# Attention's output projection as seven products over token and head halves, in a two-layer retention and stick-breaking decoder on one Trainium2 core

## The chip, the core and the metric

The kernel runs on one core of one Trainium2 chip. A core has five engines that work side by side, each through its own instructions in order: TensorE (PE in the profile, with its weight loads as PEld), VectorE (DVE), ScalarE (ACT), GpSimd (POOL) and SyncE (SP), which here only issues DMAs. Matrix products land in eight PSUM banks of 128 x 512 float32; all else lies in SBUF, or in DRAM, from where DMAs bring it. The metric is the time on the device in microseconds, as a median of several runs. A profile is one execution, so its numbers belong to that execution's own time.

## What is computed

The input is 1024 tokens of width 1024. Layer 0 is retention with four heads, layer 1 is stick-breaking attention with eight heads of 256 values. Only the end of layer 1 matters here (cut from the reference):

```python
u = rms_norm(h, sb_norm_pre[j])
proj = u @ sb_w_in[j]
q, g = jnp.split(proj, [SB_QK_WIDTH], axis=-1)
q = split_heads(q, SB_HEADS).astype(jnp.float32)
o = stick_breaking_attention(q, k_shared, v_shared)
o = merge_heads(o).astype(h.dtype) * jax.nn.silu(g)
y = o @ sb_w_out[j]                      # 1024 x 2048 by 2048 x 1024
h = h + rms_norm(y, sb_norm_post[j])
```

`stick_breaking_attention` gives each token a sum over all earlier tokens, so a token of the upper half looks at both halves, and token 0 gets zero. `y = o @ sb_w_out` is the output projection.

## The kernel before

Float32 products are made of three matmuls: each operand is split into a high part (ACT rounds it to the fast format) and a low part (DVE subtracts), and `mm3` adds high x high, high x low and low x high in a PSUM bank. So each operand of a product costs a half on ACT and a half on DVE before PE can use it.

Tokens go in two halves `t` (0 lower, 1 upper) of 512. The attention heads go in pairs `p` (0 to 3). `CPair` holds one pair of heads for one token half; `rows(hh)` makes the scores of one head (sigmoids, a scan and a product on DVE), `mix(hh)` transposes the weights on PE, splits them and multiplies them by the values into two banks `po`, and its last step `gate` multiplies by the gate.

Ahead of the heads stand six groups of input products, K, Q, V0, G0, V1 and G1 (`Group`). Each computes a 1024 x 1024 block by seven products of 48 matmuls over halves of tokens and inputs (numbers 1 to 7; number 2 of all six groups is made first). V1 and G1 are values and gates of heads 4 to 7.

The output projection of layer 1 is made per pair. The gate's result is split into tiles `oT` in SBUF, and `outproj` (lower tokens, result with the output's columns on the partitions) or `outproj_rows` (upper tokens, result in rows) multiplies it by the pair's quarter of the weights: 8 banks of 4 blocks of the inner dimension, 3 matmuls each, 96 per call. The sums over pairs are kept in DRAM (`y_d`): loaded into `f`, added to a bank, stored again. Each call stands beside a later head pair, so that PE has these matmuls while ACT and DVE work on the head. The first pair of the lower half stands beside G1's last two products, the second pair beside nothing, and the last pair's call, upper tokens, ends the kernel. `c_post` norms the lower half with statistics from PE and writes it; `finish` norms the upper half by rows as its banks come.

The output projection of layer 0 is different: `AOut` makes it from seven products of four quarters each way (the Winograd form of Strassen's method). A product has four units `i`; a unit has a weight tile `whl` and an operand tile `op`, both of 128 x 2 x 1024, which `weights` and `operand` make from one to three quarters loaded from DRAM as `raw`, added or subtracted on DVE and split; PE uses a unit for 24 matmuls.

The order in time is not that of the code: all instructions are recorded, and a planner (`Plan`) with a cost for each places them on the engines, within the dependencies and the numbers of buffers. `merge` sets which work is recorded beside which. Nearly all instructions carry one line of a recorder (L229 in the profile), so they are told apart by the names of their tiles: `pma`, `pmb`, `pz` and `po` are PSUM banks (two each), `wraw`/`raw` loaded weights, `whl` split weights, `A` weights of attention, `AT` their split transposes, `ko`, `v`, `vo` keys, queries and values, `sg` gates, `f` scratch.

Of the kernel before, what the change touches and what calls it, by code (L numbers as in the profile page):

```python
# [10 lines left out]
F32 = mybir.dt.float32  # L11
# [446 lines left out]
def trunk(ctx, tc, xT, wts, gains, trig, ident_in, cols, grow_in, out):  # L458
# [64 lines left out]
    def unit(idx, gain=None):  # L523

        w = S("whl", [2, 1024], F32R)
        for c in range(2):
            o = 512 * c
            raw = S("wraw", [512])
            dma(raw[:], wts[idx, :, o:o + 512])
            for a, b, g in [(p[0] - o, p[1] - o, p[2]) for p in gain if o <= p[0] < o + 512] if gain else [(0, 512, None)]:  # L530
                split((w[:, 0, o + a:o + b], w[:, 1, o + a:o + b]), raw[:, a:b], g)
        return w

# [34 lines left out]

    def proj(base, xh, typ, evac, gain=None):


        box = {}
        get = ahead(4, lambda kk: unit(base + kk, gain(kk) if gain else None))

        def chunk(j):
            kk, half, c = j // 4, j // 2 % 2, j % 2
            i = 2 * kk + c
            if j == 0:
                box["b"] = [PS(n) for n in banks4]
            w, x, banks = get(kk), xh[i], box["b"]  # L580
            if j % 4 == LEAD:
                get(kk + 1)
            for b in (2 * half, 2 * half + 1):
                bl = slice(128 * b, 128 * b + 128)
                if typ == "N":
                    n = slice(512 * c + 128 * b, 512 * c + 128 * b + 128)
                    mm3(banks[b][:], w[:, 0, n], w[:, 1, n], x[:, 0, :], x[:, 1, :], i == 0, i == 7)
                else:
                    n = slice(512 * c, 512 * c + 512)
                    mm3(banks[b][:], x[:, 0, bl], x[:, 1, bl], w[:, 0, n], w[:, 1, n], i == 0, i == 7)  # L590
            if j >= 12 and c:
                evac(2 * half, banks)

        return Chunks([lambda j=j: chunk(j) for j in range(16)], lambda: get(0))

    def outproj(base, oT, y_d, first, acc=None, tags=None, hold=None):

        box = {}
        get = ahead(4, lambda ng: unit(base + ng))

        def sum_so_far(c):
            if hold is None:
                y = S("f2", [512])
            else:
                if c < 4:
                    hold.append(S("S", [2, 512]))
                y = hold[c % 4][:, c // 4]
            if not first:
                dma(y[:], y_d[c])
            return y  # L610
        sums = ahead(8, sum_so_far)

        def chunk(j):
            c, half = divmod(j, 2)
            ng, b = divmod(c, 2)
            w = get(ng)
            if j % 4 == LEAD:
                get(ng + 1)
            if half == 0:
                box["p"] = PS(tags[c % 4] if tags and c < 4 else banks4[c % 4])  # L620
                sums(c)
                if not first:
                    sums(c + 1)
                    sums(c + 2)
            p, y = box["p"], sums(c)
            for e in (2 * half, 2 * half + 1):
                n = slice(256 * e + 128 * b, 256 * e + 128 * b + 128)
                mm3(p[:], w[:, 0, n], w[:, 1, n], oT()[e][:, 0, :], oT()[e][:, 1, :], e == 0, e == 3)
            if half == 0:
                return  # L630
            if first:
                A_.activation(y[:], p[:], AF.Copy)
            else:
                V.tensor_tensor(y[:], p[:], y[:], ALU.add)
            if hold is None:
                dma(y_d[c], y[:])
            if acc is not None:
                sumsq(acc, y[:], c, G if hold is None else V)

        def pre():  # L640
            get(0)
            if not first:
                sums(0)
                sums(1)

        return Chunks([lambda j=j: chunk(j) for j in range(16)], pre)

    def outproj_rows(base, oT, y_d, first, done=None):

        box = {}  # L650
        get = ahead(4, lambda u: unit(base + u))

        def sum_so_far(c):
            y = S("f2", [512])
            if not first:
                dma(y[:], y_d[c])
            return y
        sums = ahead(8, sum_so_far)

        def chunk(j):  # L660
            c, half = divmod(j, 2)
            nh, tb = divmod(c, 4)
            w = get(2 * nh + half)
            if tb == 2:
                get(2 * nh + half + 1)
            if half == 0:
                box["p"] = PS(banks4[c % 4])
                sums(c)
                if not first:
                    sums(c + 1)  # L670
                    sums(c + 2)
            p, y, tl = box["p"], sums(c), slice(128 * tb, 128 * tb + 128)
            for e in range(2):
                x, n = oT()[2 * half + e], slice(512 * e, 512 * e + 512)
                k = 2 * half + e
                mm3(p[:], x[:, 0, tl], x[:, 1, tl], w[:, 0, n], w[:, 1, n], k == 0, k == 3)
            if half == 0:
                return
            if first:
                A_.activation(y[:], p[:], AF.Copy)  # L680
            else:
                V.tensor_tensor(y[:], p[:], y[:], ALU.add)
            if done:
                done(nh, tb, y)
            else:
                dma(y_d[c], y[:])

        def pre():
            get(0)
            if not first:  # L690
                sums(0)
                sums(1)

        return Chunks([lambda j=j: chunk(j) for j in range(16)], pre)
# [80 lines left out]
    y_d = [[rec.tile(dr, [128, 512], F32, f"y{t}{c}", dram=True) for c in range(8)] for t in range(2)]  # L775
# [6 lines left out]
    v_d = [[[DRAM(f"v{t}{p}{b}", F32R) for b in range(4)] for p in range(NPAIR)] for t in range(2)]  # L782
    g_d = [[[rec.tile(dr, [128, 512], F32, f"g{t}{p}{f}", dram=True) for f in range(4)] for p in range(NPAIR)] for t in range(2)]
# [285 lines left out]
    class AOut:  # L1069

        def __init__(self, base, hold, acc):
            self.base, self.hold, self.acc = base, hold, acc
# [33 lines left out]
        def operand(self, n, i):  # L1106

            def load(t, half):
                raw = S("raw", [1024])
                dma(raw[:], o_d[t][2 * half + i // 2][i % 2][:])  # L1110
                return raw

            x = S("op", [2, 1024], F32R)
            if n in (1, 2, 3):
                a = load(*{1: (1, 0), 2: (1, 1), 3: (0, 1)}[n])
            elif n in (5, 7):
                a, b = (load(1, 0), load(0, 0)) if n == 5 else (load(0, 1), load(0, 0))
                V.tensor_tensor(a[:], a[:], b[:], ALU.subtract)
                if n == 5:
                    self.x[i] = a  # L1120
            else:
                a, b = self.x[i], load(0, 1) if n == 6 else load(1, 1)
                V.scalar_tensor_tensor(a[:], a[:], -1.0, b[:], ALU.mult, ALU.subtract)
            split(self.pieces(x), a[:])
            return x

        def put(self, t, j, b, y):
            sumsq(self.acc[t], y, 4 * j + b, V)
# [26 lines left out]
        def y(self, t, j, b):  # L1155
            if self.hold[t][b] is None:
                self.hold[t][b] = S("S", [2, 512])
            return self.hold[t][b][:, j]

        def chunk(self, n, i, kk):  # L1160
# [6 lines left out]
            w, x = self.get(at)  # L1167
            banks = self.banks[5 if n == 3 else n]
            sl = slice(512 * kk, 512 * kk + 512)
            for b in range(4):  # L1170
                cl = slice(512 * kk + 128 * b, 512 * kk + 128 * b + 128)
                mm3(banks[b][:], w[:, 0, cl], w[:, 1, cl], x[:, 0, sl], x[:, 1, sl], n != 3 and i + kk == 0, i == 3 and kk == 1, goes_on=n == 3)
            if i == 3 and kk == 1:
                for b in range(4):
                    self.done(n, b, banks[b])
# [340 lines left out]
    class CPair:  # L1516
        def __init__(self, t, pr):
            self.t, self.pr, self.base, self.off = t, pr, 112 + 16 * t + 4 * pr, HT * t
            self.oT = [None] * 4
            self.A = [[], []]  # L1520
            self.kq = [None] * 4

        def out(self, y_d, acc=None, done=None):
# [398 lines left out]
```

## Time and profile before

| | |
|---|---|
| median of three runs | 1617.39 us (1615.33 to 1618.29) |
| the profiled execution, its own time | 1614.99 us |
| its span, first to last instruction | 1613.2 us |
| mean granted TensorE clock | 0.999 |
| DRAM traffic | 405.85 MB, 252 GB/s over the span |
| DMA landing, median | `wraw` 5.0 us, `ko` 6.1 us, `raw` 7.2 us |

The profile's views used here: the page (busy time of each engine, and 40 slices of the span in tenths), the waits (who waited for whom), windows (busy time in given stretches), the chain of work that ended last, the groups of equal instructions (count, busy us, mean ns of one, idle time before), the timeline, and the DMA issues. The ends of matmuls are modelled, so the start of one to the start of the next tells their pace.

### The profile page before, as it was taken

To read this page: it belongs to the slowest core of one execution; us is meant where nothing else is said; L and a number is where in the kernel's file an instruction comes from. 1 tells how busy PE (TensorE), PEld (TensorE's weight loads), DVE (VectorE), ACT (ScalarE), POOL (GpSimd) and SP (SyncE) were. 2 spreads that over 40 slices of the span, in tenths; PEclk is the share of its full clock that TensorE was granted. 3 is DMA by queue.
4 is the path that set the end of the run, shared out by engine and by line. 5 is a ranking of instruction groups with operands and counts; after the bars stand their busy time and mean duration, and the time that the engine had idled before them with its cause. 6 is when DMAs were issued, how large, how long until landed. Compare 5 with 4: busy or idle time off the path is not lost.

```text
span 1613.2 us, 22605 instructions
## 1 busy us (share of the span) xinstructions
PE 1600.7 (99%) x7538; PEld 1327.9 (82%) x7538; DVE 1275.5 (79%) x1942; ACT 829.1 (51%) x1490; POOL 238.4 (15%) x306
## 2 busy tenths in 40 slices
PE   9999999999999999999999999999999999999997
PEld 7888888888888888888788888888888888888886
DVE  7998779787667787899978765757758886878997
ACT  7643432323566665545665554545545645545543
POOL 0000024240122323300000000000002211212410
PEclk9999999999999999999999999999999999999999
DMA  8775636478557887885676967659787878787893
GB/s 284 245 254 173 228 111 229 137 270 291 178 194 272 302 320 270 306 309 185 223 271 222 347 227 280 243 176 317 259 318 263 272 250 302 258 297 266 286 301 129
DMA packets 187573, 405.85 MB, mean 252 GB/s; under 512 B 21057, under 2 KB 21697, under 8 KB 187457
## 3 DMA queue, kind: packets, MB, share of 16 engines
q1 hardware_dynamic: 187456, 404.41, 71.9%
q8 instruction: 59, 0.97, 0.2%
q14 instruction: 58, 0.47, 0.1%
HBM read 291.08 MB, written 113.25 MB: 251 GB/s over the span
## 4 chain that ended last, share of the span: by engine, by line
PE 74%; DVE 2%; issue 1%; POOL 1%; ACT 1%; DMA 0%; DVEq 0%; SPq 0%; POOLq 0%; ACTq 0%
PE pma L229 21%; PE pmb L229 20%; PE po L229 18%; PE pz L229 15%; DVE f L229 1%; DMA wraw<-in_wts_dram 0%; DVE S L229 0%; POOL f L229 0%; POOL small L229 0%; DVE acc L229 0%; ACT f L229 0%; DVE small L229 0%; ACT sgn L229 0%; DVE wraw L229 0%; ACT whl L229 0%
## 5 line engine op out<-in xcount | busy, mean ns | idle before, releaser
L229 ACT ACTIVATE whl<-wraw 128x512 fp32r<-128x512 f32 (+1 forms) x328 | 194.3, 626 | 240.3 <-PE po L229 73.0
L229 DVE TENSOR_TENSOR whl<-wraw,whl 128x512 fp32r<-128x512 f32 x328 | 228.5, 722 | 108.8 <-ACT whl L229 108.0
L229 PE MATMUL pma<-whl,xh 128*128 128x512 f32 x480 | 125.3, 393 | 0.4 <-ACT whl L229 0.4
L229 PE MATMUL pmb<-whl,xh 128*128 128x512 f32 x480 | 122.7, 389 | 0.0
L229 POOL TENSOR_SCALAR_AFFINE_SELECT f<-f 128x128 f32<-128x128 f32 x64 | 32.9, 531 | 504.5 <-ACT f L229 493.7
L229 PE MATMUL pma<-xh,whl 128*128 128x512 f32 x408 | 105.7, 392 | 0.2 <-ACT xh L229 0.2
L229 PEld LDWEIGHTS pmb<-whl,xh 128*128 128x128 f32 x480 | 90.0, 188 | 18.9
L229 PE MATMUL pmb<-xh,whl 128*128 128x512 f32 x408 | 104.6, 391 | 0.0
L229 PEld LDWEIGHTS pma<-whl,xh 128*128 128x128 f32 x480 | 88.6, 188 | 18.3 <-ACT whl L229 0.8
L229 PE MATMUL pz<-ko,ko 128*128 128x512 f32 (+3 forms) x480 | 101.7, 331 | 0.0
L229 POOL TENSOR_TENSOR f<-f,f 128x512 f32<-128x512 f32 x32 | 56.0, 1759 | 248.5 <-DVE f L229 222.5
L229 DVE SCALAR_TENSOR_TENSOR wraw<-wraw,gn,wraw 128x512 f32<-128x512 f32 x96 | 70.4, 748 | 24.9 <-ACT wraw L229 18.8
L229 PEld LDWEIGHTS pma<-xh,whl 128*128 128x128 f32 x408 | 75.9, 188 | 17.0 <-ACT xh L229 0.8
L229 PEld LDWEIGHTS pmb<-xh,whl 128*128 128x128 f32 x408 | 76.5, 188 | 16.2 <-issue 0.5
L229 PE MATMUL pma<-op,whl 128*128 128x512 f32 x336 | 89.5, 396 | 0.0
L229 PE MATMUL pmb<-op,whl 128*128 128x512 f32 x336 | 86.1, 390 | 0.0
L229 PEld LDWEIGHTS pz<-ko,ko 128*128 128x128 f32 x480 | 77.4, 189 | 9.9 <-DVE AT L229 0.9
L229 PE MATMUL pma<-whl,oT 128*128 128x512 f32 x312 | 82.2, 397 | 0.5 <-ACT whl L229 0.5
L229 PE MATMUL pmb<-whl,oT 128*128 128x512 f32 x312 | 80.4, 392 | 0.0
L229 ACT ACTIVATE AT<-pz 128x512 fp32r<-128x512 f32 (+1 forms) x96 | 45.9, 491 | 65.0 <-PE pz L229 64.8
L229 PE MATMUL po<-xh,whl 128*128 128x512 f32 x312 | 79.2, 389 | 0.0
L229 PE MATMUL pz<-xh,whl 128*128 128x512 f32 x312 | 79.1, 389 | 0.0
(213 smaller groups left out, 3588.2 us busy)
## 6 DMA issues: line engine op xcount, KB each, us to landing
wraw<-in_wts_dram SPq DMA_DIRECT2D x495, 256.0 KB, 5.0
v<-v SPq DMA_DIRECT2D x64, 512.0 KB, 6.0
ko<-kq SPq DMA_DIRECT2D x40, 512.0 KB, 6.1
raw<-in_wts_dram SPq DMA_DIRECT2D x36, 512.0 KB, 7.2
raw<-o SPq DMA_DIRECT2D x36, 512.0 KB, 7.3
kq<-v SPq DMA_DIRECT2D x32, 512.0 KB, 6.3
y<-f SPq DMA_DIRECT2D x56, 256.0 KB, 2.9
f<-y SPq DMA_DIRECT2D x48, 256.0 KB, 4.8
```

Of the source, the lines that this page charges most:

```text
L229: f(*[_real(a) for a in o.args], **{k: _real(v) for k, v in o.kw.items()})
```

## The change

The projection of layer 1 becomes one call of the class that layer 0 used, renamed `Out`: seven products over token halves and head halves (heads 0 to 3 lower, 4 to 7 upper). `gate` no longer splits its result; it writes it to DRAM (`oc_d`), from where `operand` loads quarters. The running sums `y_d`, `outproj`, `outproj_rows` and `c_post` go. Operands are `turned`, so that both token halves come out in rows, and `finish(t)` now norms both; for token 0 it sets the factor to zero. The last product, number 2, runs bank by bank (`last`) where the others run all four banks for each unit.

The heads are recorded in another order: the eight lower head calls (two halves of tokens, heads 0 to 3) stand beside four products each of V1 and G1 (numbers 6, 7, 4, 5), and the eight upper ones beside products 1, 5, 3 and 6 of the projection, two each. Products 7, 4 and 2 come after the last head.

```diff
-    def outproj(base, oT, y_d, first, acc=None, tags=None, hold=None):
...
-    def outproj_rows(base, oT, y_d, first, done=None):
...
+    oc_d = [[[DRAM(f"oc{t}{p}{n}", F32) for n in range(2)] for p in range(NPAIR)] for t in range(2)]
...
-    class AOut:
+    class Out:
...
-                dma(raw[:], o_d[t][2 * half + i // 2][i % 2][:])
+                dma(raw[:], self.o_d[t][2 * half + i // 2][i % 2][:])
...
+            if n == 2 and self.turned:
+                x = [hl("AT") for _ in range(2)]
+                for kk in range(2):
+                    split((x[kk][:, 0], x[kk][:, 1]), a[:, 512 * kk:512 * kk + 512])
+                return x
...
+        def multiply(self, n, i, kk, b, bank):
+            w, x = self.get(self.units.index((n, i)))
+            w, x = w[:, :, 512 * kk:512 * kk + 512], x[kk]
+            l, r = (x, w) if self.turned else (w, x)
+            cl = slice(128 * b, 128 * b + 128)
+            mm3(bank[:], l[:, 0, cl], l[:, 1, cl], r[:, 0, :], r[:, 1, :], n != 3 and i + kk == 0, i == 3 and kk == 1, goes_on=n == 3)
+            if i == 3 and kk == 1:
+                self.done(n, b, bank)
...
+        def last(self):
+            first = self.units.index((2, 0))
+
+            def chunk(b, i):
+                if b == 0:
+                    self.get(first + i)
+                    self.get(first + i + 1)
+                if i == 0:
+                    self.banks[b] = PS(banks4[b])
+                for kk in range(2):
+                    self.multiply(2, i, kk, b, self.banks[b])
+            return Chunks([lambda b=b, i=i: chunk(b, i) for b in range(4) for i in range(4)], lambda: self.get(first))
...
             def gate():
+                o = S("S", [2, 512])
                 for e in range(2):
-                    j = 2 * hh + e
-                    g = box["g"][e]
-                    V.tensor_tensor(g[:], box["po"][e][:], g[:], ALU.mult)
-                    if e == 0:
-                        self.o = S("oT", [2, 2, 512], F32R)
-                    x = self.oT[j] = self.o[:, e]
-                    split((x[:, 0, :], x[:, 1, :]), g[:])
+                    V.tensor_tensor(o[:, e], box["po"][e][:], box["g"][e][:], ALU.mult)
+                dma(oc_d[self.t][self.pr][hh][:], o[:].rearrange("p a b -> p (a b)"))
...
-    def c_post(t, y_d, acc):
...
-    def finish():
+    def finish(t):
...
+            if t + tb == 0:
+                seen = S("small", [1])
+                V.tensor_scalar(seen[:], ident[:, 0:1], -1.0, 1.0, ALU.mult, ALU.add)
+                V.tensor_tensor(r[:, 0:1], r[:, 0:1], seen[:], ALU.mult)
...
-        heads = [(0, 0), (0, 1), (1, 0), (0, 2), (1, 1), (0, 3), (1, 2), (1, 3)]
-        fill = [None, (0, 0), (0, 1), (1, 0), (0, 2), (1, 1), (0, 3), (1, 2)]
...
+        heads = [(0, 0), (0, 1), (1, 0), (1, 1), (0, 2), (0, 3), (1, 2), (1, 3)]
+        P = {h: CPair(*h) for h in heads}
+        seq = [(h, hh) for h in heads for hh in range(2)]
...
+        for at, first in ((4, 0), (5, 4)):
+            n = order[at]
+            go(groups[at].chunks(n[0]), None if first else lambda: [(P[seq[0][0]].rows(0), 0, 0)])
+            for k in range(4):
+                go(groups[at].chunks(n[k + 1]), lambda k=k: head(first + k))
+            go(groups[at].chunks(n[5]))
+        turns, done = zip(*[finish(t) for t in range(2)])
+        Y = Out(112, oc_d, True, lambda t, j, b: S("f2", [512])[:], lambda t, j, b, y: done[t](j, b, y))
+        for k, n in enumerate((1, 5, 3, 6)):
+            for half in range(2):
+                go(Y.chunks(n)[4 * half:4 * half + 4], lambda k=k, half=half: head(8 + 2 * k + half))
+        go(Y.chunks(7), lambda: [(turns[0], 0, 1)])
+        go(Y.chunks(4), lambda: [(turns[1], 0, 0)])
+        go(Y.last())
```

Where instructions come to stand is seen from the built program's order, which has no times. First PE at the very end. Before, the last two banks (`pmb`), each 12 matmuls from two weight tiles and the last pair's two `oT` tiles:

```order
L229 MATMUL pmb_15879<-whl_15705,oT_15471 128x512 x6
L229 MATMUL pmb_15879<-whl_15728,oT_15755 128x512 x6
L229 MATMUL pmb_15902<-whl_15705,oT_15471 128x512 x6
L229 MATMUL pmb_15902<-whl_15728,oT_15755 128x512 x6
```

Now the very last bank alone, over four weight tiles and the eight half operands of product 2:

```order
L229 MATMUL pmb_15637<-whl_15341,AT_15357 128x512 x3
L229 MATMUL pmb_15637<-whl_15341,AT_15370 128x512 x3
L229 MATMUL pmb_15637<-whl_15391,AT_15413 128x512 x3
L229 MATMUL pmb_15637<-whl_15391,AT_15419 128x512 x3
L229 MATMUL pmb_15637<-whl_15452,AT_15469 128x512 x3
L229 MATMUL pmb_15637<-whl_15452,AT_15475 128x512 x3
L229 MATMUL pmb_15637<-whl_15485,AT_15515 128x512 x3
L229 MATMUL pmb_15637<-whl_15485,AT_15519 128x512 x3
```

A bank now takes 24 matmuls in a row where it took 12.

Second, SP where the second head of the upper tokens' third pair is loaded: its own keys, its queries and the lower tokens' keys, all into `ko`. Before (`y_91` is a running sum's store, `wraw` and `vo` are weights and values for later):

```order
L229 DMA wraw_14178<-in_wts_dram 128x512
L229 DMA ko_14189<-kq_242 128x1024
L229 DMA y_91<-f_13784 128x512
L229 DMA ko_14219<-kq_244 128x1024
L229 DMA ko_14237<-kq_226 128x1024
L229 DMA vo_14260<-v_259 128x512
```

Now the same three loads (queries, lower keys, own keys), among them the store of the gated head before (`oc_272`):

```order
L229 DMA raw_13857<-oc_270 128x1024
L229 DMA ko_13880<-kq_228 128x1024
L229 DMA oc_272<-S_13873 128x1024
L229 DMA ko_13914<-kq_210 128x1024
L229 DMA ko_13927<-kq_226 128x1024
L229 DMA v_13937<-v_257 128x1024
```

The two loads of keys now stand behind a store that waits for DVE's gating of a head. On PE, between that head's last product (`po`) and the first use of the keys, now stand 32 matmuls of 512 columns and 8 transposes, the last of them these:

```order
L229 MATMUL pz_13916<-ident,A_13888 128x128
L229 MATMUL po_13951<-AT_13947,vo_13768 128x512
L229 MATMUL po_13954<-AT_13947,vo_13768 128x512
L229 MATMUL pz_13959<-ko_13914,ko_13880 128x512 x3
L229 MATMUL pz_13966<-ko_13927,ko_13880 128x128 x3
```

The last two rows are the scores that use the loaded keys.

Third, DVE at the end of product 4, where its first banks (`pma_15238`, `pma_15248`) are read and the operands of product 2 are made:

```order
L229 SCALAR_TENSOR_TENSOR A_15102<-A_15102,col_15444,A_15090 128x1024
L229 SCALAR_TENSOR_TENSOR A_15068<-A_15068,col_15446,A_15124 128x1024
L229 TENSOR_TENSOR whl_15452<-raw_15397,whl_15452 128x1024
L229 SCALAR_TENSOR_TENSOR f_15480<-pma_15238,f_14957 128x512
L229 SCALAR_TENSOR_TENSOR f_15487<-pma_15248,f_14970 128x512
L229 TENSOR_TENSOR AT_15469<-raw_15416,AT_15469 128x512
L229 TENSOR_TENSOR AT_15475<-raw_15416,AT_15475 128x512
L229 TENSOR_TENSOR whl_15485<-raw_15437,whl_15485 128x1024
```

Before, DVE near its end read a bank, scaled it, and wrote a row block for each bank in turn, with nothing else between:

```order
L229 TENSOR_TENSOR f_15659<-pma_15837,f_15659 128x512
L229 TENSOR_TENSOR A_15780<-f_15659,A_15481 128x512
L229 RECIPROCAL col_15872<-small_15866 128x1
L229 SCALAR_TENSOR_TENSOR A_15780<-A_15780,col_15872,A_15535 128x1024
L229 TENSOR_TENSOR f_15678<-pma_15857,f_15678 128x512
```

Now the lower tokens' finish (`A_15102`, `A_15068`), the reading of product 4's banks and the halves of product 2's operands share DVE.

More of the change, by code (lines that the diff above doesn't have):

```diff
@@ L567, in ahead @@
         return get
[L569 to L594, printed above, removed]
@@ L596, in outproj @@
-    def outproj(base, oT, y_d, first, acc=None, tags=None, hold=None):
[L598 to L646, printed above, removed]
@@ L648, in outproj_rows @@
-    def outproj_rows(base, oT, y_d, first, done=None):
[L650 to L694, printed above, removed]
@@ L1166, in chunk @@
                     self.banks[n] = [PS(tag) for tag in banks4]
[L1167 to L1169 removed]
             for b in range(4):
[L1171 to L1175, printed above, removed]
+                self.multiply(n, i, kk, b, self.banks[5 if n == 3 else n][b])
         def chunks(self, *which):
@@ new lines, in run @@
+        for at, group in enumerate(groups[:4]):
+            go(group.chunks(*order[at]), (lambda: [(late[2:], 0, 16)]) if at == 0 else None)
+        for at, first in ((4, 0), (5, 4)):
[5 more added lines that the diff above has]
+        turns, done = zip(*[finish(t) for t in range(2)])
```

179 lines of the change are left out of this document (47 added, 132 removed).

## The prediction

> **What bounds the kernel now.** I read the page first, for the busy shares and the slices.
>
> ```profile
> span 1613.2 us, 22605 instructions
> PE 1600.7 (99%) x7538; PEld 1327.9 (82%) x7538; DVE 1275.5 (79%) x1942; ACT 829.1 (51%) x1490; POOL 238.4 (15%) x306
> PE   9999999999999999999999999999999999999997
> PEclk9999999999999999999999999999999999999999
> ```
>
> PE has work in every slice but the last, at a clock that is never throttled. A busy PE need not be at its peak, so next come the waits of PE (what it waited for, total us, times, longest) and windows in stretches where no head runs (us; then busy us and instruction count of PE, PEld, DVE, ACT, POOL; clock, DMA share, GB/s).
>
> ```profile
> PE pz L229 <- DVE onesr L229: 1.4, 1, 1.4
> PE po L229 <- ACT sgn L229: 1.1, 3, 0.4
> PE pma L229 <- ACT whl L229: 1.0, 2, 0.5
> ...
> 960.00:1000.00 40.00, 40.00 (x178) 33.13 (x177) 28.51 (x45) 21.13 (x37) 0.00 (x0) 1.00 0.94 347
> 1120.00:1200.00 80.00, 80.00 (x354) 66.16 (x354) 50.74 (x78) 40.90 (x70) 0.00 (x0) 1.00 0.82 293
> ```
>
> All waits of PE come to 4.0 us in 1613. In 80 us 354 matmuls start, one per 0.226 us. The chain that ended last (start us, length, what) has the same pace in its tail, and the price of a transpose:
>
> ```profile
> 1582.09 0.90 PE pz L229 x8
> 1582.99 5.51 PE pma L229 x24
> 1588.49 5.44 PE pmb L229 x24
> ```
>
> 24 matmuls of 512 columns take 5.44 us, 0.227 each; eight 128x128 transposes take 0.90, 0.113 each. So the time is a sum of matmuls that follow each other, with a head and a tail. A change is worth what it takes off that sum, unless PE starts to wait.
>
> **The change on PE.** The old projection has eight head pairs (four, each for two token halves), each with 8 banks of 12 matmuls: 768. Seven products of 96 are 672. Removed: 96 x 0.227 = 21.8 us. Lower tokens now end in rows, as upper ones did, so the residual of that half is turned: 32 more transposes x 0.113 = 3.6 us. Its old statistics go:
>
> ```profile
> L229 PE MATMUL pz<-ones,acc 128*128 128x1 f32 x56 | 6.7, 241 | 0.3 <-DVE acc L229 0.3
> L229 PE MATMUL pz<-sgn,onesr 128*128 128x512 f32 x10 | 3.8, 392 | 0.0
> ```
>
> Four products with ones, 8 of these 56 records at 6.7/56 = 0.12 us: 1.0; and two of `sgn,onesr` at the pace of 512 columns, 0.45. PE's sum falls by 21.8 + 1.0 + 0.45 - 3.6 = **19.6 us**. The heads, with their scores, transposes and value products, are the same sixteen, and only stand elsewhere.
>
> The Trainium skill has a rule that would make this smaller: "TensorE: Matmul & The Clock Gate", section "Back-to-back issue gap", gives about 131 ns for a 512-column matmul in a sustained stream. By it the 96 would be worth 12.6 us, and the time about 1607. This trace does not agree: it has 227 ns, 24 times in a row.
>
> **The tail.** Rows of the timeline (start us, length, engine, operation, count, idle before):
>
> ```profile
> 1599.21 5.60 PE L229 MATMUL pmb<-whl,oT 128*128 128x512 f32 x24
> 1605.10 0.75 DVE L229 SCALAR_TENSOR_TENSOR f<-f,col,A 128x512 f32<-128x512 f32 x1
> 1605.77 0.68 DVE L229 TENSOR_TENSOR f<-pmb,f 128x512 f32<-128x512 f32 x1
> 1607.83 1.41 DVE L229 SCALAR_TENSOR_TENSOR f<-f,col,A 128x512 f32<-128x512 f32 x2
> ```
>
> PE is done at 1604.81, but the last bank is read 0.96 us later, since DVE still writes the rows of the bank before; banks end 2.7 us apart (12 matmuls), and a bank's chain on DVE and ACT takes 1609.24 - 1605.77 = 3.5. In the changed order a bank has 24 matmuls, 5.4 us, so that chain is over. The rest (the same chain, the same two 256 KB stores) stays: **-0.9 us**.
>
> **Waits that may come.** (a) Loads. The order of the instructions has two loads of K behind the store of a gated head, and 32 matmuls of 512 columns and 8 transposes, 32 x 0.227 + 8 x 0.113 = 8.2 us, from that head's last product to their use. What has to fit in: two gate multiplications, the loads' own issue, the landing:
>
> ```profile
> L229 DVE TENSOR_TENSOR sg<-po,sg 128x512 f32<-128x512 f32 x32 | 21.2, 681 | 1.2 <-PE po L229 1.1
> L229 SPq DMA_DIRECT2D ko<-kq x34: 320/406/973, 1200.9 to 1514.1; - x34
> DMA to landing us min/median/max: 3.6/5.8/9.1
> ```
>
> 2 x 0.68 + 0.41 + 5.8 = 7.6 by the median, and 10.9 by the longest landing. So from nothing (0.6 to spare) to 2.7 late; nearer to the median, I take **+0.5**. The store itself is queued between them, another 0.4. Behind the waiting store SP also holds value loads, used more than 10 us later. Before, the same load had 28 us: the store ahead of it, `y_91`, belongs to a bank that ended that much PE work earlier.
>
> (b) DVE. Per instruction:
>
> ```profile
> L229 DVE TENSOR_TENSOR whl<-wraw,whl 128x512 fp32r<-128x512 f32 x328 | 228.5, 722 | 108.8 <-ACT whl L229 108.0
> L229 DVE TENSOR_TENSOR whl<-raw,whl 128x1024 fp32r<-128x1024 f32 x28 | 34.2, 1225 | 6.1 <-ACT whl L229 6.1
> L229 DVE TENSOR_TENSOR op<-raw,op 128x1024 fp32r<-128x1024 f32 x28 | 34.0, 1218 | 6.8 <-ACT op L229 6.7
> L229 DVE TENSOR_TENSOR raw<-raw,raw 128x1024 f32<-128x1024 f32 x24 | 29.4, 1224 | 0.0
> L229 DVE TENSOR_TENSOR oT<-sg,oT 128x512 fp32r<-128x512 f32 x32 | 22.8, 719 | 0.1
> L229 DVE TENSOR_TENSOR f<-pma,f 128x512 f32<-128x512 f32 x62 | 42.2, 687 | 13.2 <-PE pma L229 13.0
> ```
>
> New: 28 + 24 long halves and 32 long sums and differences, 84 x 1.22 = 102 us, and 20 for the turned operands and the second finish. Gone: 64 weight halves (46), 32 of `oT` (23), 28 additions to running sums (19), and some 17 of the old finish. DVE gains 17 us, (1275.5 + 17) of about 1594: 81%, no bound over the whole. By place: an upper-token head costs DVE (means of its groups)
>
> ```profile
> L229 DVE TENSOR_TENSOR_SCAN sgn<-sgn 128x640 f32<-128x640 f32 (+3 forms) x32 | 61.2, 1914 | 16.4 <-POOL sgn L229 16.3
> L229 DVE TENSOR_TENSOR A<-A,sgn 128x639 f32<-128x639 f32 (+3 forms) x32 | 34.7, 1083 | 0.7
> L229 DVE TENSOR_TENSOR AT<-pz,AT 128x512 fp32r<-128x512 f32 (+1 forms) x96 | 51.7, 550 | 20.3 <-ACT AT L229 19.9
> ```
>
> 4 x 1.91 + 4 x 1.08 + 8 x 0.55 + 2 x 0.68 = 17.8 us, and PE 16.2 (9984 columns of scores and 19968 of values, 13.3 at 0.227 for 512, and 26 transposes, 2.9), plus 48 matmuls of the product beside it, 10.9: 27.1. Beside a product of G1 DVE adds 50.74/80 of 10.9, 6.9: 24.7 of 27.1. Beside product 3 it adds two units, each two halves and two sums, 2 x 4.9: 27.6 of 27.1. In product 4, which ends the work without heads, the rows count 13 long (1.22) and 16 short (0.69) instructions: 27.3 us against PE's 96 x 0.227 + 32 x 0.113 = 25.4. But means are upper bounds, since such instructions overlap: five in 3.26 us, 0.65 each, where the mean is 0.72. And PE stood a DVE that was nearly full:
>
> ```profile
> 1578.74 3.26 DVE L229 TENSOR_TENSOR whl<-wraw,whl 128x512 fp32r<-128x512 f32 x5 [0.83 <-ACT whl L229]
> 1520.00:1560.00 40.00, 40.00 (x215) 33.93 (x214) 37.88 (x51) 20.69 (x42) 14.35 (x15) 1.00 0.88 293
> ```
>
> A tenth less puts all three under PE's time. Product 4's cost is 0 to 1.9, product 3's 0 to 1.0 (two heads): I take **+0.5** for both, near the overlapped end.
>
> (c) Units fed from DRAM. The retention projection already runs the same 28 units:
>
> ```profile
> L229 PE MATMUL pma<-op,whl 128*128 128x512 f32 x336 | 89.5, 396 | 0.0
> L229 PE MATMUL pmb<-op,whl 128*128 128x512 f32 x336 | 86.1, 390 | 0.0
> ```
>
> PE never waited there: 0 here.
>
> **Sum.** -19.6 - 0.9 + 0.5 + 0.5 = -19.5. The profiled execution took 1614.99 us, so it would take 1595.5. It was 2.4 under the median of the runs shown, 1617.39, so the median would be **1598**. Their spread is 1615.3 to 1618.3; a measurement of this kernel can tell about 0.2% (3.2 us) from no change.
>
> **Rivals.** 1. *Late operands in the last stretch.* All upper ends of (a) and (b) at once: 2.7 + 1.9 + 1.0 in place of 1.0, with a second load of K (10.5 us ahead) also late by 0.4: 1603, and up to 1607. For it: the margins are under 1 us. Against: the load must take the longest of 34 landings.
> 2. *Transfers bound product 7.* It takes 16 loads and 4 of the residual, 20 x 0.524 MB = 10.5 MB in its 25.4 us, 413 GB/s. The row of 347 GB/s at a share of 0.94 makes 369 GB/s at full use: 28.4 us, 3.0 late, so 1601. Against: the program's order issues its first unit's loads beside the last head, and six microseconds of the trace ran faster:
>
> ```profile
> 1196.00:1202.00 6.00, 6.00 (x28) 4.99 (x27) 2.51 (x5) 4.40 (x8) 0.00 (x0) 1.00 1.02 409
> ```
>
> The Trainium skill, "DMA: Bandwidth & Descriptors", section "Where 436 GB/s comes from", sets about 358 GB/s for a core's traffic with HBM; by it the product would take 29.3 us and be 3.9 late. The 409 GB/s of the row above shows that it is no ceiling on one core alone, if only for 6 us.
> 3. *Slower: DVE bounds all eight upper-token heads.* Price: in the `whl<-wraw` row each half waits 108.8/328 = 0.33 us for ACT's half; 16 such halves a head (8 `AT`, 8 of a product) make 5.3 us. If none of it is covered, 24.7 + 5.3 = 30.0 against 27.1, 2.9 a head, 23 in all, and 34 with a fourth more beside products 3 and 6, where DVE starts from 27.6: 1621 to 1632. It decides for the worse from 2.4 us of uncovered waits a head on (no gain from about 4.8). Against: the window with DVE at 37.88 of 40.
> 4. *The sum moves but the time doesn't*: half of case 3, some 17 to 20 us given back in many small waits: 1615.
>
> **Chances.** Forecast, 1594 to 1601: 0.70. Rival 1: 0.15; rival 2: 0.06; rival 3: 0.05; rival 4: 0.04. Faster 0.91, within 0.2% 0.04, slower 0.05. Range 1593.5 (lowest run, no new wait) to 1607 (rival 1 at its end), which leaves out rivals 3 and 4.
>
> **What would show it.** PE at 9 in all slices, its waits still about 4 us, 96 fewer 512-column records: right. `ko` among what PE waits for by over 1 us: (a) missized. A wait of PE on `whl`, `op` or `AT` after the last head: rival 1 or 2, told apart by whether DVE is full or DMA at 1.0. DVE at 10 tenths with PE under 9 beside the heads: rival 3. A last bank read more than 0.2 us after PE's end: the tail is wrong.

## The result and the profile after

| | before | after |
|---|---|---|
| median of the runs, us | 1616.47 (1615.33 to 1618.29) | **1599.2** (1597.94 to 1599.68) |
| ratio, 95% interval | | 0.9891, 0.9874 to 0.9908 |
| span of the profiled execution, us | 1613.2 | 1596.2 |
| PE from the span's start to its last matmul's end, us | 1604.81 | 1589.61 |
| from there to the span's end, us | 8.4 | 6.6 |

The change takes off 17 us, 1.1%. The forecast was 1598. From the page of the changed kernel:

```profile
span 1596.2 us, 22335 instructions
PE 1583.0 (99%) x7464; PEld 1314.4 (82%) x7464; DVE 1299.1 (81%) x1911; ACT 831.0 (52%) x1470; POOL 218.1 (14%) x298
PE   9999999999999999999999999999999999999998
PEclk9999999999999999999999999999999999999999
```

PE is at 9 to the end and its clock stands. It has 74 matmul records fewer, just what the count says: 98 of 512 columns (96 of products and two of `sgn`) and eight with ones less, 32 transposes more. DVE gained 23.6 us, where 17 were expected. What PE waits for (total us, times, longest), the rows over 0.5:

```profile
PE po L229 <- ACT AT L229: 1.8, 3, 0.6
PE pz L229 <- DVE onesr L229: 1.4, 1, 1.4
PE pz L229 <- DVE acc L229: 0.8, 1, 0.8
PE pz L229 <- DVE A L229: 0.7, 1, 0.7
PE pma L229 <- ACT whl L229: 0.6, 1, 0.6
PE po L229 <- ACT sgn L229: 0.6, 1, 0.6
```

No `ko`, no `op`, no DMA. New are the waits for `AT` and `A`, the operands of a head. Windows show where they are (us; busy us and instructions of PE, PEld, DVE, ACT, POOL; clock, DMA share, GB/s). First the changed kernel:

```profile
1240.00:1280.00 40.00, 39.42 (x206) 32.77 (x205) 31.46 (x37) 24.06 (x50) 9.46 (x12) 1.00 0.74 251
1400.00:1440.00 40.00, 38.69 (x199) 31.84 (x198) 38.10 (x38) 24.70 (x45) 11.22 (x12) 1.00 0.80 279
1440.00:1480.00 40.00, 39.36 (x203) 32.86 (x202) 35.29 (x35) 21.50 (x42) 4.76 (x10) 1.00 0.75 263
1545.00:1570.00 25.00, 25.00 (x128) 20.72 (x127) 24.87 (x35) 19.03 (x37) 0.00 (x0) 1.00 0.57 211
```

The same time in the kernel before:

```profile
1400.00:1440.00 40.00, 40.00 (x215) 33.74 (x214) 30.71 (x45) 18.44 (x40) 8.10 (x14) 1.00 0.85 294
```

PE is idle for 1.31 and 0.64 us between 1400 and 1480, with DVE at 38.10 of 40 in the first of these windows. By the matmul records product 3, beside the two heads of the pair (1, 2), runs from 1406 to 1465, product 7 from 1517 to 1542, and product 4 from there to 1567. In product 4 DVE is fuller still (24.87 of 25), and PE does not wait. The timeline of the first of these stalls (start us, length, engine, operation, count, idle before):

```profile
1405.77 2.02 DVE L229 TENSOR_TENSOR_SCAN sgn<-sgn 128x896 f32<-128x896 f32 x1
1407.70 1.25 DVE L229 TENSOR_TENSOR raw<-raw,raw 128x1024 f32<-128x1024 f32 x1
1408.87 2.37 DVE L229 TENSOR_TENSOR_SCAN sgn<-sgn 128x1024 f32<-128x1024 f32 x1
1411.17 2.19 DVE L229 TENSOR_TENSOR A<-A,sgn 128x895 f32<-128x895 f32 x2
1413.42 0.44 PE L229 MATMUL pz<-ident,A 128*128 128x128 f32 x2 [0.70 <-DVE A L229]
1414.43 0.73 PE L229 MATMUL po<-AT,vo 128*128 128x512 f32 x2 [0.58 <-ACT AT L229]
1415.16 1.24 PE L229 MATMUL pz<-ko,ko 128*128 128x512 f32 x6
```

DVE runs without a gap: a scan, an addition of weights, the last scan, the rows of `A`; PE gets the transposes of `A` 0.70 us late and the products that follow them 0.58 late. The end of the kernel, in the same columns:

```profile
1585.82 3.79 PE L229 MATMUL pmb<-whl,AT 128*128 128x512 f32 x16
1589.64 0.69 DVE L229 TENSOR_TENSOR f<-pmb,f 128x512 f32<-128x512 f32 x1 [2.02 <-PE pmb L229]
1591.65 1.42 DVE L229 SCALAR_TENSOR_TENSOR A<-A,col,A 128x512 f32<-128x512 f32 x2
```

DVE now waits for the last bank (2.02 us) and reads it as it ends.

**Where the 17.0 us of the span come from.** PE's stretch is 15.2 us shorter, where its sum fell by 19.6, so waits and restarts grew by 4.4; the stretch behind PE is 1.8 shorter. To place the 4.4, take from the matmul records the time from each start to the next, less the pace of that kind of matmul (0.227 for 512 columns, 0.113 for a transpose), and sum it by stretch. This *lost pace* holds idle time and the slower matmuls at a restart, in us:

| kernel | 1200 to 1280 | 1360 to 1480 | 1480 to 1600 |
|---|---|---|---|
| before | 1.7 | 1.5 | 1.5 |
| after | 2.5 | 4.6 | 1.1 |
| e1_after, the same again | 2.5 | 4.6 | 1.1 |
| e9_after, the same again | 2.6 | 6.2 | 1.2 |
| e3_relief | 2.5 | 1.9 | 2.7 |
| e4_spread | 2.5 | 2.7 | 3.0 |
| e5_gpsimd | 2.4 | 15.9 | 1.5 |
| e7_less3 | 2.5 | 12.6 | 1.1 |
| e10_early | 2.5 | 3.8 | 1.5 |
| e11_half | 2.5 | 4.6 | 1.3 |
| e12_eight | 2.5 | 1.3 | 1.0 |

After 1080 us it is 5.6 before and 10.5 after. A few tenths in a cell hang on the exact paces and on where a stretch is cut. The experiments ask what the 5 us are, whether the sum is worth its pace, and what makes the tail.

### The profile page after: what moved, and what is told of

It is laid out like the page before. It is cut to its first block, busy times and chain, and to the rows that moved or that the text cites. A ratio compares the mean times of both kernels' runs of the same rounds, so it can differ in the third digit from the quotient of the medians.

```text
span 1596.2 us, 22335 instructions
## 1 busy us (share of the span) xinstructions
PE 1583.0 (99%) x7464; PEld 1314.4 (82%) x7464; DVE 1299.1 (81%) x1911; ACT 831.0 (52%) x1470; POOL 218.1 (14%) x298
## 4 chain that ended last, share of the span: by engine, by line
PE 74%; DVE 2%; DMA 1%; ACT 1%; issue 1%; POOL 1%; DVEq 0%; SPq 0%; POOLq 0%; ACTq 0%
PE pma L229 21%; PE pmb L229 21%; PE po L229 18%; PE pz L229 15%; DVE f L229 0%; DMA wraw<-in_wts_dram 0%; DVE S L229 0%; POOL f L229 0%; ACT sgn L229 0%; DVE sgn L229 0%; DMA raw<-in_wts_dram 0%; DVE acc L229 0%; POOL small L229 0%; DMA v<-v 0%; DVE wraw L229 0%
## 5 line engine op out<-in xcount | busy, mean ns | idle before, releaser
L229 ACT ACTIVATE whl<-wraw 128x512 fp32r<-128x512 f32 (+1 forms) x264 | 157.6, 626 | 236.1 <-PE po L229 70.2
L229 DVE TENSOR_TENSOR whl<-wraw,whl 128x512 fp32r<-128x512 f32 x264 | 186.3, 730 | 90.6 <-ACT whl L229 90.2
L229 PE MATMUL pz<-ko,ko 128*128 128x384 f32 (+3 forms) x480 | 99.5, 332 | 0.3 <-ACT A L229 0.2
L229 ACT ACTIVATE op<-raw 128x1024 fp32r<-128x1024 f32 x52 | 55.2, 1062 | 45.6 <-PE pmb L229 19.2
L229 PE MATMUL pma<-whl,op 128*128 128x512 f32 x288 | 77.8, 398 | 0.0
```

What stands on the lines that cost most here:

```text
L229: f(*[_real(a) for a in o.args], **{k: _real(v) for k, v in o.kw.items()})
```

## The experiments

All are edits of the changed kernel. Times are medians.

**e1_after, the control.**

> The changed kernel again, as a control on the same chip as the three variants sent with it. All theories: 1597 to 1601 us, ratio to before 0.988 to 0.991.

1600.22 us, ratio to before 0.9902 (0.9887 to 0.9917). A third set, e9_after below, gave 1600.31. Differences under about 2 us between sets are not read as such.

**e2_tail, the last product unit by unit.**

```diff
-        go(Y.last())
+        go(Y.chunks(2))
...
-            if n == 2 and self.turned:
+            if False:
```

> The last product unit by unit, as the other six are (96 matmuls in bank turns of 3), in place of bank by bank. All else as in the changed kernel. Theory (the tail is the chain of the banks behind PE's last matmul): the four banks then end 0.68 us apart instead of 5.4, each has some 2.6 us of VectorE behind it, so three banks queue up ahead of the last chain: the stretch behind PE's last matmul grows from 6.6 us by 4 to 8, and the time goes to 1603 to 1607. Rival (the tail is only the landing of the last stores, whatever the order): 1599, within 1 us.

1604.91 us, 4.7 more than the control. Its end:

```profile
1589.24 1.52 PE L229 MATMUL pmb<-whl,op 128*128 128x512 f32 x6
1590.64 1.28 DVE L229 TENSOR_TENSOR f<-pmb,f 128x512 f32<-128x512 f32 x2
1596.31 2.72 DVE L229 SCALAR_TENSOR_TENSOR A<-A,col,A 128x512 f32<-128x512 f32 x4
```

Its operands come whole here, as in the other six products, and no longer as halves. PE ends at 1590.76 and the span at 1602.9: 12.2 us for 6.6. DVE works for 8.3 us behind PE, where the changed kernel has 3.5. So the order of the last product is worth about 5 us: taken like the other six, it would have eaten more than a quarter of the gain.

**e3_relief, product 3's sums left out.**

```diff
-                a = plus(self.s[i], load(0, 0))
-                a = plus(load(0, 1), a)
+                if self.turned:
+                    load(0, 0)
+                    a = load(0, 1)
+                else:
+                    a = plus(self.s[i], load(0, 0))
+                    a = plus(load(0, 1), a)
```

> Leaves out part of the computation: eight of VectorE's long additions (1.22 us each) that make the weights of product 3, which stands beside the two heads of one pair of upper tokens. Their loads are all kept. Theory (VectorE, whose order puts these sums ahead of the heads' scans and row products, is just in time there, and PE's extra waits of some 4 us beside upper-token heads come of it): PE's idle time between 1400 and 1490 us, 2.0 us now, falls to under 1, and the time by 1 to 3 us, to 1596 to 1598. Rival (the loads, or the heads' own chain over ScalarE, hold PE up): no change, 1599 within 0.7. No theory moves the stretch ahead of 1400 us, where the instructions stay as they are.

1597.51 us, 2.7 less than the control. The windows:

```profile
1400.00:1440.00 40.00, 40.00 (x210) 33.78 (x209) 32.72 (x33) 25.47 (x46) 8.60 (x12) 1.00 0.76 275
1440.00:1480.00 40.00, 39.89 (x208) 33.18 (x207) 33.93 (x36) 20.61 (x41) 4.94 (x10) 1.00 0.84 300
1520.00:1560.00 40.00, 38.97 (x194) 31.89 (x194) 35.54 (x46) 22.27 (x39) 0.00 (x0) 1.00 0.76 294
```

With 9.8 us less on DVE and the same loads, the 1.95 us of idle PE become 0.11, and the lost pace of that stretch goes from 4.6 to 1.9. The stretch ahead of 1400 stays as it was. The planner also moved things behind it, which brought 1.03 us of idle into product 7 and 1.6 of lost pace behind 1480, so that by the records 1.1 us are left over; the medians say 2.7, with sets of one kernel about 1 us apart. DVE's extra sums are the cause of the waits beside product 3; the loads aren't.

**e4_spread, the last four heads over three products.**

```diff
-        for k, n in enumerate((1, 5, 3, 6)):
+        for k, n in enumerate((1, 5)):
...
-        go(Y.chunks(7), lambda: [(turns[0], 0, 1)])
+        three = Y.chunks(3, 6, 7)
+        for k in range(4):
+            go(three[6 * k:6 * k + 6], lambda k=k: head(12 + k) + ([(turns[0], 0, 1)] if k == 3 else []))
```

> The last four heads over three products (3, 6 and 7) instead of two (3 and 6): 72 matmuls beside each head in place of 48, and the turned residual of the first token half beside the last head. Theory (VectorE just in time beside the upper-token heads): PE has 5.4 us more of cover for each head, waits between 1400 and 1490 us go from 2.0 to under 1, and the time to 1596.5 to 1598.5, a version faster than both. Against it: product 4, alone at the end with VectorE at 24.87 of 25 us, gets none of VectorE's slack that product 7 held now; if this decides, a new wait of 1 to 4 us in product 4 and 1600 to 1603.

1599.47 us, not told apart from the control; the expectation failed. PE's idle between 1400 and 1480 fell only to 1.06, 0.34 came after it, and a wait of 0.8 for `op` in the last stretch: the lost pace of the two last columns, 5.7 in all, stayed 5.7. More cover doesn't help where the cover itself costs DVE as much as it gives PE: a unit of product 3 has 4 x 1.22 = 4.9 us of DVE for 24 x 0.227 = 5.4 of PE. With three units in place of two beside the first head, DVE has 17.8 + 14.7 = 32.5 us for PE's 16.2 + 16.3 = 32.5.

**e5_gpsimd, product 3's sums on GpSimd.**

```diff
+                eng = G if self.turned else V
-                a = plus(self.s[i], load(0, 0))
-                a = plus(load(0, 1), a)
+                a = plus(self.s[i], load(0, 0), eng)
+                a = plus(load(0, 1), a, eng)
```

> The same eight long additions of product 3's weights, kept, but on GpSimd instead of VectorE (nothing is left out). GpSimd is busy 14% and its additions of 128x512 take 1.73 us in the profile of the changed kernel, so one of 128x1024 should take about 3.5 us, eight 28 us. Theory (VectorE's order is what PE waits for between 1400 and 1480 us): VectorE loses 9.8 us there, the waits of 1.95 us in those windows fall under 1, and the time by 0.5 to 2 us against the changed kernel's 1599.2 and 1600.2, a version faster than both. Rival (VectorE slows down beside a busy GpSimd, or the additions come too late for product 3): VectorE's rows of 128x1024 over 1.3 us, or a new wait on whl in product 3; 1600 to 1604.

1611.21 us; the ratio to before is 0.9970 (0.9958 to 0.9981), so nearly 12 us of the 17 are lost. The rival came, with both of its mechanisms and at three times its price. GpSimd's and DVE's rows of the timeline:

```profile
1394.20 6.41 POOL L229 TENSOR_TENSOR raw<-raw,raw 128x1024 f32<-128x1024 f32 x2 [0.45 <-DMA raw<-in_wts_dram]
1395.02 3.33 DVE L229 TENSOR_TENSOR op<-raw,op 128x1024 fp32r<-128x1024 f32 x1
1399.07 2.22 DVE L229 TENSOR_TENSOR A<-A,sgn 128x639 f32<-128x639 f32 x1
1412.56 3.30 DVE L229 TENSOR_TENSOR A<-A,sgn 128x895 f32<-128x895 f32 x1
```

Beside GpSimd's addition, DVE's `op` half takes 3.33 us (1.22 else) and `A` 2.22 and 3.30 (0.81 and 1.07 else). DVE got no relief: over the whole run it was busy for 1302.3 us, where the changed kernel had 1299.1 with the 9.8 us of sums. PE was idle for 9.1 us between 1360 and 1480; the longest waits, twice 2.04 us, were for DVE's `whl` half in product 3, which came too late. The Trainium skill, "GPSIMD Engine Reference", section "Specifications", says that GpSimd and VectorE share their way into SBUF and collide where a VectorE instruction reads two inputs from SBUF; these rows agree. `AT<-pz,AT`, which reads one input from PSUM, kept its 0.68 us beside such an addition.

**e6_less4 and e7_less3, 32 matmuls less.** One matmul in three of product 4, and of product 3.

```diff
         kw = dict(skip_group_check=True) if goes_on else {}
+        if two:
+            MM(p, lh, rh, start=start, stop=False, **kw)
+            MM(p, ll, rh, start=False, stop=stop, **kw)
+            return
```

> Leaves out one of the three matmuls of each triple of product 4 (32 of 512 columns, 7.3 us at 0.227). All operands, loads and additions are kept. Theory by the sum of matmuls: the full 7.3 us, 1592.4. Rival (VectorE, at 24.87 of 25 us beside product 4, is the second bound there): PE waits on whl or op, and only 0.5 to 3 us come off, 1597 to 1599.

> Leaves out one of the three matmuls of each triple of product 3, beside the first two heads of upper tokens in the last pair but one (32 matmuls, 7.3 us of PE). Theory by the sum alone: 7.3 us less, 1592.4. Theory of VectorE just in time there: it has 27.6 us of work by the means for PE's 27.1 beside each head, so with 3.6 us less of PE it becomes the bound: PE's waits between 1400 and 1490 us grow from 2 to 5 or more and the time falls by only 0 to 3.5 us, to 1596 to 1599.5.

e6_less4: 1592.17 us (ratio 0.9854, 0.9839 to 0.9869), 7.0 to 8.1 less than the three sets of the changed kernel: the full 7.3. In product 4 DVE is not a second bound, though it is busy for 17.90 of the 18 us from 1542 on: PE does not wait there, where no head stands whose next step hangs on DVE's last result. e7_less3: 1600.07 us (0.9901, 0.9888 to 0.9915), nothing of the 7.3. Its windows:

```profile
1400.00:1440.00 40.00, 36.88 (x186) 30.56 (x185) 37.67 (x37) 25.90 (x46) 9.91 (x12) 0.96 0.73 262
1440.00:1480.00 40.00, 36.69 (x183) 29.70 (x182) 33.50 (x34) 19.78 (x39) 4.96 (x11) 0.96 0.80 279
```

PE idles 6.4 us where it idled 1.95, and the lost pace grew by 8.0, somewhat more than was taken away; the expectation, 0 to 3.5 us off, is met at its lower end. But of the 8.0 only 4.5 are new waits, 3.5 of them for rows of `A` from DVE. Most of the rest is the clock, at 0.96 in both windows: it fell to 0.50 for 3.4 us at 1415.2 and again at 1445.9, which costs PE half of 6.8, 3.4 us. So beside product 3 a matmul less was worth nothing here, because of waits, mostly for DVE, and because the clock fell after them.

**e8_twice1, 96 matmuls more.** Product 1 is done twice.

```diff
+            two = self.turned and n == 1
...
+            if two:
+                mm3(bank[:], l[:, 0, cl], l[:, 1, cl], r[:, 0, :], r[:, 1, :], False, i == 3 and kk == 1)
```

> Adds 96 matmuls of 512 columns where no operand is added: each triple of product 1 is done twice (its result is twice what it should be). It puts back on PE what the change took away, without the old projection's loads, additions or rows. Theory by the sum: 21.8 us more, 1621 to 1622. Rival (part of the 17 us came from the moved heads or from the tail, and matmuls cost less than their pace since PE waits anyway): under 19 us more.

1619.71 us (ratio 1.0026, 1.0016 to 1.0036), 19.4 to 20.5 more than the three sets of the changed kernel. Between the two theories' numbers, and nearer to the sum: beside product 3, which now runs from 1432 to 1490, PE's idle time is 0.97 where it was 1.95, and the lost pace from 1080 on is about 1.2 lower. That DVE could work ahead beside the longer product 1 would explain it; no run shows it.

**e10_early and e11_half, the sums made earlier.** e10_early makes the sum for product 5 beside product 1, and the first sum for product 3 beside product 5; e11_half only the second.

```diff
             split(self.pieces(w), a[:])
+            if self.turned and n == 1:
+                self.s[i] = plus(load(1, 0), load(1, 1))
+            if self.turned and n == 5:
+                plus(self.s[i], load(0, 0))
             return w
```

> The changed kernel once more, as a control on the same chip as the two variants sent with it: 1598 to 1601 us.

> Nothing is left out; VectorE keeps all its additions, but eight of 1.22 us are made earlier: the sum of the two weights that product 5 uses beside product 1, and the sum that product 3 starts from beside product 5. Long operations of VectorE per unit of products 1, 5, 3, 6 go from 2, 4, 4, 3 to 3, 4, 3, 3. Theory (the place where VectorE is full, beside product 3 and the first upper-token pair, sets PE's waits there; it had 31 to 33 of 40 us beside product 1): between 1400 and 1480 us PE's idle time of 1.95 us falls under 1, VectorE's 38.1 of 40 in the first of these windows falls by 2 or more, and the time by 1 to 2.5 us against the control: 1597 to 1599, faster than both kernels. Rival (the earlier loads and held buffers cost as much elsewhere, or the heads' own chain sets the waits): within 0.7 of the control.

> The second of these two moves alone: the sum that product 3 starts from (four of 1.22 us) beside product 5, where VectorE has 37.9 of 40 us in the windows from 1320; long operations per unit of products 1, 5, 3, 6: 2, 5, 3, 3. Theory: the waits between 1400 and 1480 us shrink as with both moves, but VectorE is now overfull beside product 5, so a new wait of 0.5 to 2 us comes between 1320 and 1400; the time within 1 us of the control, and slower than with both moves. Rival (only the total of VectorE beside the last two head pairs counts): as fast as with both moves.

Control 1600.31, e10_early 1598.9 (ratio 0.9896, 0.9881 to 0.9911), e11_half 1599.01 (0.9901, 0.9885 to 0.9917; the control's is 0.9898). No difference can be told. e10_early's window:

```profile
1400.00:1440.00 40.00, 38.83 (x200) 32.34 (x199) 39.13 (x39) 24.43 (x46) 10.64 (x12) 1.00 0.87 310
```

The expectation that DVE would empty by 2 us failed: it is at 39.13, and PE still idles 1.17 us there and none in the next window. With half of the sums gone from the place, the planner put other work of DVE into it. The lost pace of e10_early fell by 0.8 from 1360 to 1480, and rose by 0.4 behind it. e11_half brought a wait beside product 5, just under the expected size (0.45 us of idle between 1360 and 1400), still idled for 1.46 us in the window after it, and won nothing. Whether e10_early is faster by about 1 us stays open.

**e12_eight, the order without the seven products.** Eight plain products, each of 4 units of a weight and an operand without sums.

```diff
+        def where(self, n):
+            return (n % 4) // 2, n % 2, n // 4
...
-        for k, n in enumerate((1, 5, 3, 6)):
+        for n in range(4):
             for half in range(2):
...
-        go(Y.chunks(7), lambda: [(turns[0], 0, 1)])
-        go(Y.chunks(4), lambda: [(turns[1], 0, 0)])
+        go(Y.chunks(4), lambda: [(turns[0], 0, 1)])
+        go(Y.chunks(5))
+        go(Y.chunks(6), lambda: [(turns[1], 0, 1)])
```

> The order of the change without its seven products: heads where the changed kernel has them, gated heads through DRAM, upper and lower rows ended alike, but the projection as eight plain products of 96 matmuls with no sums or differences of operands (four of lower heads beside the upper heads, then four of upper heads, the last bank by bank). Nothing is left out. PE's sum is that of the changed kernel plus 96 matmuls, 21.8 us, so 2.2 above the one before. Theory (the 17 us come from the 96 matmuls alone, less some 3 to 4 us of waits that VectorE's extra sums cause beside upper-token heads): those waits go, as VectorE has 22.7 us for PE's 27.1 beside such a head, and the time is 1599.7 + 21.8 - 3.5 = 1618, within 1616 to 1620. Rival 1 (the new order of heads or the row form saves time by itself): 1613 or less. Rival 2 (the order itself is what brings the new waits, whatever VectorE adds): PE's idle time between the first upper-token head and the last stays at 3 us or more, and 1621 to 1624.

1620.59 us (ratio 1.0030, 1.0018 to 1.0043): slower than before by 4.6. By time alone it lies between the theory's 1620 and rival 2's 1621; the windows decide:

```profile
1240.00:1280.00 40.00, 39.42 (x202) 32.68 (x201) 32.21 (x39) 24.20 (x49) 8.95 (x10) 1.00 0.78 269
1400.00:1440.00 40.00, 40.00 (x212) 34.06 (x211) 30.89 (x31) 22.06 (x43) 12.16 (x14) 1.00 0.71 263
1440.00:1480.00 40.00, 40.00 (x209) 33.50 (x209) 30.76 (x32) 23.41 (x44) 7.72 (x10) 1.00 0.65 227
```

No idle beside the last heads, with DVE at 31 of 40. So rival 2 falls, and so does rival 1: the order and the row form save nothing. Against the kernel before, e12_eight has 2.2 us more of matmuls, 1.5 more of lost pace from 1080 on and 1.0 more behind PE, 4.7 in all. What remains between 1240 and 1280, 0.58 us of idle, is the same in all kernels with the new order, and belongs to it. The excess over 1618 is a tail of my own making:

```profile
1601.75 1.06 ACT L229 ACTIVATE op<-raw 128x1024 fp32r<-128x1024 f32 x1 [10.22 <-PE pmb L229]
1606.18 3.79 PE L229 MATMUL pmb<-whl,op 128*128 128x512 f32 x16
```

The last operand is split only at 1601.75, so all four banks end within the last 5 us in spite of their order; the span ends at 1619.3, 9.4 us behind PE in place of 6.6. With 2.7 more, 1618 becomes 1620.7.

One sentence ahead of the prediction has to be set right here: in the kernel before, the second pair did not stand beside nothing, but beside the first pair's call, and so on; only the first stood beside G1. No term of the sum rested on it.

## Why the prediction was right, and where it was not

- **PE's sum, -19.6: right.** It follows from the records' paces (from 1587.8 to 1568.2 us in all), and three runs carry it: 32 matmuls less where PE is the bound gave 7.0 to 8.1 for 7.3 (e6_less4); 96 more, in two ways, gave 19.4 to 21.4 (e8_twice1, e12_eight), with the waits that they hid and the tail that e12_eight added. By the 131 ns of the Trainium skill, "TensorE: Matmul & The Clock Gate", section "Back-to-back issue gap", the 32 would have been worth 4.2 us; the runs do not agree.
- **The tail, -0.9: the chain right, the rest mis-sized.** From PE's end to DVE's last instruction it went from 1609.24 - 1604.81 = 4.43 to 1593.07 - 1589.61 = 3.46, by 0.97. But the stores behind it also ended 0.8 sooner after DVE, which I had left as it was; the whole is -1.8. e2_tail shows that it hangs on the order of the last product.
- **(a) Loads behind the store, +0.5: 0.** PE waits for `ko` in no run. In the changed kernel the loads were issued at 1406.3 and used at 1415.16; the stall of 1.3 us lies in between, but e3_relief and e12_eight, without it, show no wait for them either.
- **(b) DVE, +0.5: the step that failed.** "A tenth less puts all three under PE's time" compared sums over a whole head. Product 4 cost 0 and not up to 1.9 (its 13 long and 16 short instructions make 26.9 us and not 27.3, so the upper end was 1.5). Product 3 cost more than its upper end of 1.0: 3.3 us of lost pace between 1360 and 1480, the difference to e12_eight, which has the same heads without the sums (3.4 from 1080 on), and 2.7 by the difference to e3_relief. DVE is not short over the two heads (73.4 us busy of the 80 from 1400 on); by the timeline it is short in the last part of a head, where the long scans, the rows of `A` and the sums follow each other without a gap, and PE's next work needs the last of them. The row `A<-A,sgn` of 1.08 us and the scan of 1.91 had hidden, as means over four shapes, that the last of a head take 1.21 and 2.37.
- **A term that was not in the sum:** the new order alone costs 1.5 us (lost pace from 1080 on: 5.6 before, 7.1 in e12_eight, 10.5 after), some 0.8 of it beside G1.
- **(c) and the rivals.** Units from DRAM cost 0; products 7, 4 and 2 run without a wait, so rivals 1 and 2 did not come, product 7 with 363 GB/s over 25 us among them:

```profile
1520.00:1545.00 25.00, 25.00 (x127) 20.85 (x127) 23.11 (x31) 17.20 (x30) 0.00 (x0) 1.00 0.94 363
```

Rival 3, DVE as the bound beside upper-token heads, came at one pair out of four, for under 4 us in place of 23.

The profiled execution took 1597.94 us by its own time, 2.4 more than the 1595.5 worked out for it: 3.4 from waits (4.4 for the 1.0 put down), less 0.9 from the tail. The median stands 1.3 above it where I had added 2.4, so of the error 1.2 us are left: two terms off in opposite directions, and some luck with the spread.

## What to carry over

Price a removed matmul at the pace of its stretch, but first ask stretch by stretch whether PE sets the time there: 32 matmuls were worth 7.3 us beside one product and, since PE then waited and its clock fell, nothing beside another some 130 us earlier. Compare the second engine with the first not over a whole step but over the last piece of it, where a chain must end before PE can go on, with the durations of the shapes that stand there. A final product is best ordered so that its banks end one after the other, which was worth 5 us here.

## What was not expected of the hardware

The clock granted to PE can fall after two short waits, and not every time. In the profiled execution of the changed kernel, after waits of 0.70 and 0.58 us, six matmuls took 1.24 us (the timeline above). The control e9_after, the same program with the same waits, had this timeline and these windows:

```profile
1419.62 0.73 PE L229 MATMUL po<-AT,vo 128*128 128x512 f32 x2 [0.58 <-ACT AT L229]
1420.34 2.10 PE L229 MATMUL pz<-ko,ko 128*128 128x512 f32 x6
```

```profile
1420.00:1422.00 2.00, 2.00 (x7) 1.37 (x6) 2.00 (x4) 1.05 (x3) 0.00 (x0) 0.62 1.03 420
1422.00:1424.00 2.00, 2.00 (x8) 1.67 (x8) 2.00 (x3) 1.38 (x4) 0.73 (x1) 0.53 0.79 258
```

The clock was at 0.50 from 1420.5 to 1423.9, 3.4 us, and at 1.00 on either side. The six took 2.10 us, and the lost pace between 1400 and 1440 was 4.3 in place of 2.7. e5_gpsimd and e7_less3, with longer waits, had two such falls each in these traces, which is 0.96 over two windows of 40 us; in all runs of these two kernels the mean clock was 0.995 to 0.997. So a new wait may cost more than its own length. The Trainium skill, "TensorE: Matmul & The Clock Gate", section "Part 1: The HAM clock gate (the "warmup" mystery)", gives half the clock after an idle window of about 3.4 us, one that runs on by itself. Half and the length agree: every fall here is to 0.50, and in each trace the changes of the clock lie whole multiples of 3.41 us apart (30.7 and 34.1 us between the falls of e7_less3 and of e5_gpsimd). That the window must be idle as a whole does not agree: in the 3.41 us ahead of the fall PE was idle for 1.3 us in e9_after, and for 1.7 to 2.4 in the other two. Nor does it help to know that both waits lay in one such window, for they did in e1_after and in e6_less4 too, again 1.3 us, and the clock stayed. What decides near 1.3 us, no run here shows.
